# VectorE, ScalarE and SyncE in source order through projections and time mixing, and attention's loads on SyncE

## Chip, cores, metric

One core of one Trainium2 chip. The metric is the device time of one execution, in us. Engines: TensorE (PE; its weight loads are PEld), VectorE (DVE), ScalarE (ACT), GpSimd (POOL), SyncE (SP, which here only issues DMAs).

## What is computed

A decoder block on x of 2048 x 1024 float32:

```python
xn = rms_norm(h, ln_attn_pre); proj = xn @ w_in            # 1792 columns time mixing, 1536 attention
y_rwkv = rwkv7_mix(proj[..., :RWKV_COLS], ...)             # 8 heads of 64; a state carried from token to token
o = diff_attention(dq, dk, dv, lam, slopes)                # 4 heads, two softmaxes each, causal, ALiBi
h = h + rms_norm(concat(y_rwkv, o) @ w_out)
u = causal_dwconv(rms_norm(h) @ w_up); h = h + rms_norm((gelu(gate) * val) @ w_down)
```

In `rwkv7_mix` the projections are first mixed with those of the token before (`shift`), decay and learning rate come from small low-rank products, keys are normalised, and the state is `state * w + sa (kk a) + v k`. The output gets a norm over each head and a gate.

## The kernel before

Matrix products run in three float32r passes (high and low parts of both sides, made by ScalarE's cast and VectorE's subtraction: `split_weight`, `transpose_half`).

**Projections** (`Proj`). `w_in` is taken in 26 blocks of 128 columns, 14 for time mixing (`NRW`) and 12 for attention (`NDF`: q, k, v of each head); tokens in two halves of two groups of 512 (`GRP`). `product` makes one block for one group, 24 matmuls in 8 steps, and after each step `pace.tick()` runs what is due. `plan` gives the order: half 0's blocks 2 to 13, half 1's 26 blocks, half 0's 12 attention blocks, and before a change of half the last two blocks as (a,0), (b,0), (b,1), (a,1). `weights` loads and splits a block when the one before it is first used. `turn` reloads normalised rows (`xr`) and transposes them for the next half. Results are written to DRAM by GpSimd (`rw`, `qq`, `kk`, `vT`).

**Time mixing** (`Rwkv.group`) is a generator for 128 tokens. Its `yield`s are offsets in ticks from its start; one group starts every `PITCH` = 34 ticks, from the product (0, 13, 1) on, so about three groups are in work at once, and there are 16. Within a group: low-rank products, scans and key norm (offsets 5 to 20); the masks, that is `M` (24, 26); its 32 x 32 blocks to DRAM (`adr`) and back (`ab`); a substitution of 31 steps on VectorE, `tmp = X * ab; X += tmp` (34 to 46, called the loop here); `X` through DRAM (`xdr`) to `x1t`, `bdx` and `M`; from `JOIN` = 64 the halves are joined (`xp`), and from 71 the state is carried over two chunks of 64 (`rp`, `sp`, `yp`, `up`); then the norm (`mp`, `vs`), the gate (`gp`) and the store to `mix`, up to offset 105. `power` makes an inverse root on GpSimd, `turned` transposes it and copies it to `rT`, `spread` multiplies `rT` out over the partitions.

**Attention** (`Attn.steps`) walks units of 128 queries of a head: `scores` of unit i and `output` of unit i - 2. K, V and Q are loaded when first needed, K and Q by GpSimd, V by SyncE. While it runs, `w_out` is loaded and split (source place: unit 6).

**Then** the output projection and the MLP, to the end.

**The order.** Every engine runs its instructions in one order. For TensorE, from the start to the end of time mixing, this is the order of the source (`tc.manual_schedule(engines={PE})`). For VectorE, ScalarE, SyncE and GpSimd, and for all engines from attention on, a planner sets it, from its own costs and the order of the source, and can draw work ahead when its tile is free. Tiles of a pool are reused one by one (`reuse_waits="tile"`).

Of the kernel before, what the change touches and what calls it, by code (L numbers as in the profile page):

```python
# [18 lines left out]
P = 128  # L19
# [58 lines left out]
def transpose_split(nc, cx, ps, xn, xh, xl, t, tag, bufs):  # L78

    g, o = divmod(t * P, GRP)  # L80
    for hf in range(2):
        transpose_half(nc, cx, ps, xn[:, hf * 512:hf * 512 + 512], xh[g], xl[g], t, hf, o, tag, bufs)
# [75 lines left out]
class Proj:  # L158


    def __init__(self, tc, nc, cx, I, pool, pace):
# [7 lines left out]
        self.x, self.w = {}, {}  # L169
# [37 lines left out]
    def rows(self, t, hf, xn, x):  # L207
        transpose_half(self.nc, self.cx, self.cx.ps, xn[:, hf * 512:hf * 512 + 512], *x, t, hf, t * P % GRP, *self.cx.ra)
# [27 lines left out]
    def turn(self, half, g, every):  # L236
# [4 lines left out]
        i = 0  # L241
        for t in range(g * 4, g * 4 + 4):
            for hf in range(2):
                xr = self.pool.tile([P, 512], F32, name=f"xr{use}_{t}_{hf}", tag="xr", bufs=3)
                nc.sync.dma_start(xr, cx.xn[half * (HALF // P) + t][:, hf * 512:hf * 512 + 512])
                transpose_half(nc, cx, cx.ps, xr, xh, xl, f"{use}_{t}", hf, t * P % GRP, *cx.mm)
                i += every
                yield i

    def weights(self, half, cb):  # L250
# [4 lines left out]
        nc.sync.dma_start(wr, self.w_in[:, :, wc * P:(wc + 1) * P])  # L255
        wh = pool.tile([P, KB, P], F32R, name=f"wh{half}_{cb}", tag="wh", bufs=2)
        wl = pool.tile([P, KB, P], F32R, name=f"wl{half}_{cb}", tag="wl", bufs=2)
        split_weight(nc, wr, wh, wl)
        self.w[half, cb] = wh, wl

    def tmp(self, n):
        pool = self.pool
        return (lambda dt: pool.tile([P, GRP], dt, name=f"e1_{n}", tag="e1", bufs=2),
                lambda dt: pool.tile([P, GRP], dt, name=f"e2_{n}", tag="e2", bufs=1))

    def shift(self, half, cb, g, pp):

        nc, cx = self.nc, self.cx
        t0 = half * HALF + g * GRP
        e1, e2 = self.tmp(f"{half}_{cb}_{g}")  # L270
        t1, xs = e1(F32), e2(F32)
        c1 = self.carry[:, cb:cb + 1]
        m1 = self.mu[:, cb:cb + 1]
        nc.scalar.activation(t1, pp, AF.Copy, scale=self.mu1[:, cb:cb + 1])
# [25 lines left out]
    def evict(self, half, cb, g, pp, n):  # L300
# [13 lines left out]
        nc.scalar.activation(hi, pp, AF.Copy, scale=sc)  # L314
        nc.vector.scalar_tensor_tensor(lo, pp, sc, hi.bitcast(F32), op0=ALU.mult, op1=ALU.subtract)
# [6 lines left out]
    def plan(self, stages):  # L322
# [3 lines left out]
        after = dict(zip(order, order[1:]))  # L326
        self.weights(*order[0])
        seen = set()
        for i, (half, blocks) in enumerate(stages):
            turns = i + 1 < len(stages) and stages[i + 1][0] != half  # L330
# [4 lines left out]
            for j, (cb, g) in enumerate(todo):  # L335
                if (half, cb) not in seen:
# [14 lines left out]
PITCH, JOIN = 34, 64  # L351
# [88 lines left out]
class Rwkv:  # L440
# [31 lines left out]
    def group(self, g):  # L472
# [19 lines left out]
        nc.sync.dma_start(vv, src[8:12, :, tok].rearrange("b p t -> p b t"))  # L492
        yield 5
# [8 lines left out]
        nc.gpsimd.tensor_tensor(k0, c4(kr), ch(v["nk_k"]), op=ALU.mult)  # L502
# [4 lines left out]
        nc.scalar.activation(tha, za, AF.Tanh, scale=0.5)  # L507
        nc.vector.tensor_scalar(th, th, 1.0, None, op0=ALU.add)
# [7 lines left out]
        sb = self.power(rn, ALU.max, 1e-24, f"kk{g}")  # L516
        pe, pc = cx.pe, T([P, 4, NC], "pc", 3)
# [3 lines left out]
        nc.vector.tensor_copy(pc, pe[:, :, :, 64])  # L521
        kt = T([P, 4, RG], "t_c")
        for hb in range(4):
            nc.scalar.activation(kt[:, hb], tha[:, hb], AF.Identity, bias=v["ka1"][:, hb:hb + 1],
                                 scale=v["kah"][:, hb:hb + 1])
        kp = kr
        tt(kp, kr, kt, op=ALU.mult)
        BK = T([P, 4, NC, 2, 64], "BK")
# [3 lines left out]
        rk = T([P, 4, RG], "t_b")  # L532
        nc.gpsimd.tensor_tensor(c4(rk), rr, ch(v["r_k"]), op=ALU.mult)
        nc.vector.tensor_scalar(tha, tha, -0.5, -0.5, op0=ALU.mult, op1=ALU.add)
# [41 lines left out]
        X = T([P, 8, 32], "X")  # L576
        nc.sync.dma_start(X, cx.xinit)
# [19 lines left out]
        for j in range(31):  # L597
            if j % 5 == 0:
                yield 34 + 2 * (j // 5)
# [60 lines left out]
        yield at  # L660
        for c in range(NC):
# [7 lines left out]
            yield at + 9 * c + 3  # L669
# [7 lines left out]
            yield at + 9 * c + 6  # L677
# [13 lines left out]
            yield at + 9 * c + 9  # L691


        at += 21
        sg = T([P, RG], "sg")
        nc.sync.dma_start(sg, src[13, :, tok])
        mp = U([P, 4, RG], "mp")
        nc.tensor.matmul(mp, cx.ones2, ybv, start=True, stop=True)
        stt(ybv, mp, -1.0 / 64, ybv, op0=ALU.mult, op1=ALU.add)
        sq = T([P, 4, RG], "t_a")  # L700
# [14 lines left out]
        yield at + 13  # L715
# [4 lines left out]
        nc.sync.dma_start(cx.mix[g * RG // GRP][0:4, :, tok].rearrange("b p t -> p b t"), ybv)  # L720
# [53 lines left out]
class Attn:  # L774


    def __init__(self, tc, nc, cx, pool, ps):
        self.tc, self.nc, self.cx, self.pool, self.ps = tc, nc, cx, pool, ps
# [9 lines left out]
    def load_k(self, h, g):  # L788
        nc, cx = self.nc, self.cx
        gs = slice(g * GRP, (g + 1) * GRP)  # L790
        ka = self.T([P, 2, GRP], "ka", f"{h}{g}", 5, F32R)
        kb = self.T([P, 2, GRP], "kb", f"{h}{g}", 5, F32R)
# [5 lines left out]
        vt = self.T([P, GRP], "vtl", f"{h}{g}", VB)  # L798
        nc.sync.dma_start(vt, cx.vT[h, :, gs])
# [4 lines left out]
        self.heads[h, g] = (ka, kb, v)  # L804

    def load_q(self, h, g):
# [5 lines left out]
        nc.gpsimd.dma_start(qa, src[0:128, :, gs])  # L812
        nc.gpsimd.dma_start(qb[0:66], src[64:130, :, gs])
        self.qs[h, g] = (qa, qb)

    def scores(self, h, qb):
        nc, cx = self.nc, self.cx
        g, qi = divmod(qb, QG // P)
        if qb % 4 == 0:
            self.load_k(h, qb // 4)  # L820
        if qi == 0:
            self.load_q(h, g)
# [42 lines left out]
        self.live[h, qb] = (E[0], sc)  # L865

# [261 lines left out]

def block_kernel(tc, I, out):
    nc = tc.nc  # L1130
    cx = Ctx()
    with ExitStack() as st:
# [18 lines left out]
        with pool("pj", "left") as pp:  # L1151
# [4 lines left out]
            with tc.manual_schedule(engines={mybir.EngineType.PE}):  # L1156
# [14 lines left out]
        banks.close()  # L1171
        cx.ps = st.enter_context(tc.tile_pool(name="ps2", bufs=4, space=PSUM, reuse_waits="tile"))
        cx.mm, cx.ra, cx.rc = ("mm", 4), ("ra", 2), ("rc", 2)
        of = OutFfn(tc, nc, cx, I, out)
# [33 lines left out]
```

## Time and profile before

| | us |
|---|---|
| three runs | 3174.24, 3181.33, 3188.11 |
| median | 3181.33 |
| profiled execution, its own time | 3190.99 |
| its span in the profile | 3189.3 |
| mean granted clock of TensorE | 0.972 of 2.4 GHz |

The projections and time mixing run from about 180 to 1086 us, attention from there to some 1530 us, output projection and MLP to the end. In the rows below, `PE x L1 <- DVE y L2` is a wait of TensorE's instruction at line 1 that writes x for VectorE's at line 2 that writes y; a wait in brackets stands before the instruction, with what ended it.

### The profile page before, as it was taken

The numbers are of one execution on the slowest core, as the hardware profiler recorded it, in microseconds if no ns is written. First come the engines' busy times: TensorE is split into PE (matmuls) and PEld (weight loads), VectorE is DVE, ScalarE is ACT, GpSimd is POOL, SyncE is SP. The second block draws the span as 40 slices with busy tenths as digits, with TensorE's granted clock in tenths as the row PEclk, the third lists the DMA queues.
The fourth block names the chain that finished last, engine by engine and source line by source line (L and its number), as shares of the span: only waits on it lengthen the run. The fifth ranks groups of instructions, "written<-read, shape, count | busy, mean of one in ns | idle before, by whom it ended". The sixth has DMA issues, their size and how long they took to land.

```text
span 3189.3 us, 46522 instructions
## 1 busy us (share of the span) xinstructions
PE 3016.8 (95%) x17411; PEld 2459.6 (77%) x17411; DVE 1937.6 (61%) x4935; ACT 1168.1 (37%) x2292; POOL 448.9 (14%) x641
## 2 busy tenths in 40 slices
PE   7998999999999789999999999999999999999998
PEld 6876777777777577778788888888887788888886
DVE  6366667576766367778455455555557455555556
ACT  5242333332432367778333322222224322222223
POOL 4211111222221334432100000000000000000002
PEclk9998999999999889999999999999999999999999
DMA  8443333434443635542444111111114311111112
GB/s 301 120 139 87 88 87 96 114 98 113 132 119 89 156 71 96 92 80 57 136 155 176 53 40 60 47 47 47 40 60 136 103 51 43 52 49 52 47 34 86
DMA packets 367075, 290.84 MB, mean 91 GB/s; under 512 B 114511, under 2 KB 317874, under 8 KB 366850
## 3 DMA queue, kind: packets, MB, share of 16 engines
q1 hardware_dynamic: 325554, 211.46, 22.7%
q0 software_dynamic: 38992, 72.21, 9.6%
q10 hardware_dynamic: 2304, 4.20, 0.3%
q8 instruction: 138, 2.26, 0.3%
q14 instruction: 87, 0.71, 0.1%
HBM read 208.91 MB, written 78.07 MB: 90 GB/s over the span
## 4 chain that ended last, share of the span: by engine, by line
PE 70%; DVE 10%; issue 7%; DMA 6%; ACT 2%; SPq 2%; POOL 2%; DVEq 0%; POOLq 0%; ACTq 0%
PE fp L103 10%; PE fp L105 10%; PE fp L104 10%; PE dn L104 5%; PE dn L103 5%; PE dn L105 5%; PE pp L293 3%; PE op L883 3%; PE pp L294 2%; PE pp L295 2%; PE po L103 2%; PE po L105 2%; PE po L104 2%; DVE xtmp L612 1%; DVE X L614 1%
## 5 line engine op out<-in xcount | busy, mean ns | idle before, releaser
L1066 DVE TENSOR_TENSOR acc<-dn,acc 128x512 f32<-128x512 f32 x320 | 211.3, 686 | 224.5 <-PE dn L105 222.1
L103 PE MATMUL fp<-f1h,uh 128*128 128x512 f32 x704 | 275.4, 391 | 5.1 <-DVE fcarry L1031 5.1
L105 PE MATMUL fp<-f1h,ul 128*128 128x512 f32 x704 | 275.2, 391 | 0.0
L104 PE MATMUL fp<-f1l,uh 128*128 128x512 f32 x704 | 275.1, 391 | 0.0
L104 PE MATMUL dn<-dl,gh 128*128 128x512 f32 x704 | 275.1, 391 | 0.0
L103 PE MATMUL fp<-f0h,uh 128*128 128x512 f32 x704 | 274.2, 389 | 0.0
L103 PE MATMUL dn<-dh,gh 128*128 128x512 f32 x704 | 272.4, 391 | 1.9 <-DVE acc L1066 1.9
L105 PE MATMUL fp<-f0h,ul 128*128 128x512 f32 x704 | 274.1, 389 | 0.0
L104 PE MATMUL fp<-f0l,uh 128*128 128x512 f32 x704 | 274.0, 389 | 0.0
L105 PE MATMUL dn<-dh,gl 128*128 128x512 f32 x704 | 264.1, 391 | 0.0
L844 DVE TENSOR_SCALAR_CACHE_REDUCE E<-sp 128x512 f32<-128x512 f32 (+3 forms) x320 | 186.1, 605 | 69.1 <-PE sp L842 37.8
L97 DVE TENSOR_TENSOR ul<-ur,uh 128x1024 fp32r<-128x1024 f32 x88 | 107.7, 1225 | 188.0 <-ACT uh L96 188.0
L1027 DVE SCALAR_TENSOR_TENSOR u<-fp,cvA,u 128x511 f32<-128x511 f32 x176 | 131.3, 746 | 120.1 <-ACT u L1025 120.1
L96 ACT CAST dh<-dr 128x1024 fp32r<-128x1024 f32 x44 | 44.4, 1047 | 385.0 <-PE dn L105 384.0
L612 DVE TENSOR_TENSOR xtmp<-X,ab 128x60 f32<-128x60 f32 (+24 forms) x496 | 109.1, 220 | 118.5 <-DMA ab<-adr 80.3
L883 PE MATMUL op<-V,at 128*128 128x128 f32 x1088 | 159.5, 288 | 9.1 <-ACT at L879 8.7
L883 PEld LDWEIGHTS op<-V,at 128*128 128x128 f32 x1088 | 144.7, 199 | 24.2 <-ACT at L879 18.4
L839 PE MATMUL sp<-ka,qa 128*128 128x512 f32 (+3 forms) x320 | 137.9, 443 | 26.4 <-DMA qa<-qq 22.8
L1025 ACT ACTIVATE u<-fp,cvB 128x512 f32<-128x512 f32 x176 | 136.5, 777 | 62.7 <-PE fp L105 62.6
L103 PEld LDWEIGHTS fp<-f1h,uh 128*128 128x128 f32 x704 | 132.7, 189 | 33.4 <-issue 5.5
L853 ACT ACTIVATE E<-E,asc 128x1024 f32<-128x1024 f32 (+7 forms) x160 | 153.4, 962 | 11.1 <-DVE asc L849 10.5
L103 PEld LDWEIGHTS dn<-dh,gh 128*128 128x128 f32 x704 | 132.6, 188 | 30.3 <-DVE acc L1066 2.3
(344 smaller groups left out, 7045.1 us busy)
## 6 DMA issues: line engine op xcount, KB each, us to landing
ur<-in_w_up SPq DMA_DIRECT2D x88, 512.0 KB
wr<-in_w_in SPq DMA_DIRECT2D x52, 512.0 KB
dr<-in_w_down SPq DMA_DIRECT2D x44, 512.0 KB
rw<-e POOLq DMA_DIRECT2D x56, 256.0 KB, 2.9
x<-in_x SPq DMA_DIRECT2D x16, 512.0 KB
xn<-x POOLq DMA_DIRECT2D x16, 512.0 KB, 6.6
xr<-xn SPq DMA_DIRECT2D x32, 256.0 KB
ab<-adr SPq DMA_DIRECT2D x64, 128.0 KB
```

What stands on the lines that cost most here:

```text
L97: nc.vector.tensor_tensor(wl, wr, wh.bitcast(F32), op=ALU.subtract)
L103: nc.tensor.matmul(out, lh(kb), rh(kb), start=(kb == 0), stop=False)
L104: nc.tensor.matmul(out, lh(kb), rl(kb), start=False, stop=False)
L105: nc.tensor.matmul(out, ll(kb), rh(kb), start=False, stop=(kb == n - 1))
L612: tt(tv, X[:, 0:n, j:j + 1].broadcast_to([P, n, w]), ab[:, j:j + 1, j + 1:32].broadcast_to([P, n, w]), op=ALU.mult)
L839: nc.tensor.matmul(sp[:, 0:n], qa[:, c, qs], ka[:, c, 0:n], start=True, stop=False)
L844: nc.vector.tensor_scalar(e[ch * GRP // EW][:, eo:eo + n], sp[:, 0:n], -1.0, None, op0=ALU.mult, op1=ALU.min, accum_out=mx[:, ch:ch + 1])
L853: nc.scalar.activation(e[i][:, 0:n], e[i][:, 0:n], AF.Exp, bias=nm, scale=-1.0, accum_out=z)
L883: nc.tensor.matmul(op, at[:, q, :], v[:, q, :], start=(kb == 0), stop=(kb == qb))
L1025: nc.scalar.activation(u, pp, AF.Identity, bias=wb(b), scale=w2(b))
L1027: stt(u[:, 1:GRP], pp[:, 0:GRP - 1], w1(b), u[:, 1:GRP], op0=ALU.mult, op1=ALU.add)
L1066: nc.vector.tensor_tensor(acc[:, t, ds_], po, acc[:, t, ds_], op=ALU.add)
```

## The change

- VectorE, ScalarE and SyncE take the order of the source too, from the product (0, 13, 1) until time mixing has ended.
- What they issue gets ticks of its own. VectorE's half of a transpose's split, of a token shift and of a q or k eviction comes one step or one tick after ScalarE's (`later`). Weights are fetched two blocks ahead and split 3 ticks after the block before is first used, or 2 ticks into the last product of a stage. `xr` is fetched two ahead. All three stages end with the order (a,0), (b,0), (b,1), (a,1). The `e2` buffers are two.
- In `group` the key product on GpSimd moves to offset 3; scans, `kt`, `kp`, BK and the masks get offsets of their own; `xinit` is loaded before the blocks go to DRAM; the loop starts at 35; `JOIN` is 59; the two chunks follow at 10 ticks; `vs` is spread at +14 in place of +12; `sg` is loaded at `JOIN` + 7; the last step stays at 105. The store to `mix` goes from SyncE to GpSimd.
- Attention's K and Q are loaded by SyncE, a unit ahead of their use, those of head 0 before the drain of time mixing; V is transposed where it was.

```diff
 def transpose_half(...):
-    nc.vector.tensor_tensor(xl[:, ks, dst], pt, xh[:, ks, dst].bitcast(F32), op=ALU.subtract)
+    return lambda: nc.vector.tensor_tensor(xl[:, ks, dst], pt, xh[:, ks, dst].bitcast(F32), op=ALU.subtract)
...
+    def later(self, at, f, *args):
+        def step():
+            f(*args)
+            yield from ()
+        self.pace.add(step(), self.pace.now + at)
...
     def shift(self, half, cb, g, pp):
         nc.scalar.activation(t1, pp, AF.Copy, scale=self.mu1[:, cb:cb + 1])
+        self.later(1, self.shifted, half, cb, g, pp, t1, xs)
...
     def plan(self, stages):
+        self.fetch(*order[0])
+        self.fetch(*order[1])
         self.weights(*order[0])
...
-            if turns:
-                a, b = blocks[-2:]
-                todo[-4:] = [(a, 0), (b, 0), (b, 1), (a, 1)]
+            a, b = blocks[-2:]
+            todo[-4:] = [(a, 0), (b, 0), (b, 1), (a, 1)]
...
-                    if (half, cb) in after:
-                        self.weights(*after[half, cb])
+                    if k + 2 < len(order):
+                        self.fetch(*order[k + 2])
+                    if cb != b:
+                        split(k + 1, 3)
+                if j == len(todo) - 1:
+                    split(place[half, b] + 1, 2)
...
-PITCH, JOIN = 34, 64
+PITCH, JOIN = 34, 59
...
+            yield 25 + 2 * c
             mv = M[:, c].rearrange("p (b e) x -> p e b x", e=2)
             for e, sx in ((0, se), (1, so)):
                 tt(mv[:, e], sx, mk, op=ALU.mult)
+        X = T([P, 8, 32], "X")
+        nc.sync.dma_start(X, cx.xinit)
...
-                yield 34 + 2 * (j // 5)
+                yield 35 + 2 * (j // 5)
...
-            yield at + 9 * c + 3
+            yield at + 10 * c + 3
...
-        yield at + 12
+        yield at + 14
         self.spread(rl, cx.rT[1])
         tt(ybv, ybv, rl, op=ALU.mult)
+        yield at + 15
...
-        nc.sync.dma_start(cx.mix[g * RG // GRP][0:4, :, tok].rearrange("b p t -> p b t"), ybv)
+        nc.gpsimd.dma_start(cx.mix[g * RG // GRP][0:4, :, tok].rearrange("b p t -> p b t"), ybv)
...
-    def load_k(self, h, g):
+    def fetch_k(self, h, g):
+        vt = self.T([P, GRP], "vtl", f"{h}{g}", VB)
+        nc.sync.dma_start(vt, cx.vT[h, :, gs])
+        if g == 0:
+            self.load_q(h, 0)
+        ka = self.T([P, 2, GRP], "kab", f"a{h}{g}", 10, F32R)
+        kb = self.T([P, 2, GRP], "kab", f"b{h}{g}", 10, F32R)
         src = cx.kk[h].rearrange("c r t -> r c t")
         for i in range(2):
-            nc.gpsimd.dma_start(ka[64 * i:64 * i + 64], src[0:64, :, gs])
-        nc.gpsimd.dma_start(kb[0:66], src[64:130, :, gs])
+            nc.sync.dma_start(ka[64 * i:64 * i + 64].bitcast(F32), src[0:64, :, gs])
+        nc.sync.dma_start(kb[0:66].bitcast(F32), src[64:130, :, gs])
...
         self.live[h, qb] = (E[0], sc)
+        h2, q2 = divmod(h * (S // P) + qb + 1, S // P)
+        if q2 % 4 == 0 and h2 < NH:
+            self.fetch_k(h2, q2 // 4)
+        if qi == 1 and q2:
+            self.load_q(h, g + 1)
...
+ORDERED = {mybir.EngineType.DVE, mybir.EngineType.Activation, mybir.EngineType.SP}
...
                     if at == (0, NRW - 1, 1):
                         for i in range(NGRP):
                             pace.add(rw.group(i), pace.now + 3 + PITCH * i)
+                        break
+                with tc.manual_schedule(engines=ORDERED):
+                    for at in products:
+                        pass
+        of = OutFfn(tc, nc, cx, I, out)
+        with pool("at", "left") as ap:
+            at = Attn(tc, nc, cx, ap)
+            at.fetch_k(0, 0)
+            with tc.manual_schedule(engines=ORDERED | {mybir.EngineType.PE}):
                 pace.drain()
```

## Rows read from the trace of the kernel before

**Rows 1.** The page, busy time: engine, busy us (share), instructions.

```profile
PE 3016.8 (95%) x17411; PEld 2459.6 (77%) x17411; DVE 1937.6 (61%) x4935; ACT 1168.1 (37%) x2292; POOL 448.9 (14%) x641
```

**Rows 2.** Windows by stage: length, busy us of each engine (instructions), clock, DMA, GB/s.

```profile
180.00:1086.00 906.00, 834.97 (x6917) 650.45 (x6917) 593.65 (x1782) 303.86 (x612) 192.61 (x238) 0.95 0.39 103
1086.00:1140.00 54.00, 25.90 (x95) 19.96 (x96) 23.23 (x73) 22.82 (x51) 21.95 (x34) 0.56 1.12 213
1140.00:1500.00 360.00, 332.88 (x2268) 284.06 (x2268) 279.31 (x1043) 267.94 (x685) 131.97 (x199) 0.97 0.41 79
...
1570.00:3189.30 1619.30, 1596.51 (x7060) 1317.63 (x7058) 919.18 (x1747) 472.58 (x739) 40.48 (x52) 0.99 0.22 70
```

**Rows 3.** TensorE's waits, 180 to 1080 us: us in total, times, longest.

```profile
PE vs L470 <- DVE rT L466: 22.6, 8, 4.3
PE rp L666 <- DVE X L614: 11.1, 7, 3.4
PE xp L641 <- DMA x1t<-xdr: 11.0, 1, 11.0
PE xt L89 <- DMA xr<-xn: 8.1, 4, 4.5
```

**Rows 4.** VectorE's waits, 180 to 1080 us.

```profile
DVE xtmp L612 <- DMA ab<-adr: 80.3, 12, 10.9
```

**Rows 5.** VectorE's groups by line, 180 to 1086 us: busy us, mean ns, idle before.

```profile
L612 DVE TENSOR_TENSOR xtmp<-X,ab 128x60 f32<-128x60 f32 (+24 forms) x496 | 109.1, 220 | 118.5 <-DMA ab<-adr 80.3 <-DMA bda<-M 13.7 <-DMA X<-xinit 12.8
L614 DVE TENSOR_TENSOR X<-X,xtmp 128x60 f32<-128x60 f32 (+24 forms) x496 | 107.6, 217 | 12.1
...
L566 DVE TENSOR_TENSOR M<-se,mask 128x512 f32<-128x512 f32 x32 | 22.0, 688 | 26.5 <-PE so L563 26.5
...
L668 DVE TENSOR_TENSOR kv<-rp,kv 128x256 f32<-128x256 f32 x32 | 13.5, 420 | 5.1 <-PE rp L666 5.1
```

**Rows 6.** Timeline, first group's loop, VectorE, then TensorE: start us, us.

```profile
217.91 0.68 DVE L566 TENSOR_TENSOR M<-so,mask 128x512 f32<-128x512 f32 x1
...
226.40 0.19 DVE L612 TENSOR_TENSOR xtmp<-X,ab 128x31 f32<-128x31 f32 x1 [4.46 <-DMA ab<-adr]
...
259.69 0.17 DVE L614 TENSOR_TENSOR X<-X,xtmp 128x8 f32<-128x8 f32 x1
...
267.92 0.60 PE L641 MATMUL xp<-ident,x1t 32*128 32x32 f32 x4 [10.99 <-DMA x1t<-xdr]
```

**Rows 7.** Timeline of the turn into attention, SyncE's queue, then TensorE.

```profile
1086.53 4.48 SPq L944 DMA_DIRECT2D wor<-in_w_out  x5
1091.12 0.86 SPq L799 DMA_DIRECT2D vtl<-vT  x2
...
1102.48 1.09 PE L802 MATMUL vp<-ident,vtl 128*128 128x128 f32 x4 [16.53 <-DMA vtl<-vT]
...
1114.49 1.05 PE L877 MATMUL tp<-ident,E 128*128 128x128 f32 x3 [0.45 <-DVE E L864]
...
1128.40 0.90 PE L839 MATMUL sp<-ka,qa 128*128 128x512 f32 x2 [7.70 <-DMA qa<-qq]
```

**Rows 8.** Timeline, first and last matmul row of the last product, TensorE.

```profile
1078.60 0.39 PE L293 MATMUL pp<-x6h,wh 128*128 128x512 f32 x1
...
1085.57 0.39 PE L295 MATMUL pp<-x6h,wl 128*128 128x512 f32 x1
```

**Rows 9.** Attention: TensorE's waits 1140 to 1500 us, and the first in time.

```profile
PE sp L839 <- DMA qa<-qq: 13.6, 3, 4.6
...
1217.80 0.76 POOL L812 DMA_DIRECT2D qa<-qq  x1 [0.18 <-issue]
...
1221.32 1.86 PE L839 MATMUL sp<-ka,qa 128*128 128x384 f32 x4 [4.55 <-DMA qa<-qq]
```

**Rows 10.** Windows of 10 us at the second head's start.

```profile
1210.00:1220.00 10.00, 5.58 (x48) 5.11 (x46) 5.15 (x17) 6.16 (x16) 5.67 (x9) 0.96 1.59 206
1220.00:1230.00 10.00, 8.69 (x51) 7.99 (x52) 2.27 (x8) 1.44 (x3) 2.89 (x5) 0.70 1.16 154
```

More of the change, by code (lines that the diff above doesn't have):

```diff
@@ L240, in turn, with fetch @@
         use = self.uses
[L241 to L250, printed above, removed]
+        rows, low = [], None
+        def fetch():
+            t, hf = g * 4 + len(rows) // 2, len(rows) % 2
+            rows.append(self.pool.tile([P, 512], F32, name=f"xr{use}_{t}_{hf}", tag="xr", bufs=3))
+            nc.sync.dma_start(rows[-1], cx.xn[half * (HALF // P) + t][:, hf * 512:hf * 512 + 512])
+        fetch()
+        fetch()
+        for i in range(8):
+            t, hf = g * 4 + i // 2, i % 2
+            if i < 6:
+                fetch()
+            do = transpose_half(nc, cx, cx.ps, rows[i], xh, xl, f"{use}_{t}", hf, t * P % GRP, *cx.mm)
+            if low:
+                low()
+            low = do
+            if i == 7:
+                low()
+            yield (i + 1) * every
+    def fetch(self, half, cb):
         nc, pool = self.nc, self.pool
@@ L255, in weights @@
         nc.sync.dma_start(wr, self.w_in[:, :, wc * P:(wc + 1) * P])
+        self.raw[half, cb] = wr
+    def weights(self, half, cb):
+        nc, pool = self.nc, self.pool
+        if (half, cb) not in self.raw:
+            self.fetch(half, cb)
         wh = pool.tile([P, KB, P], F32R, name=f"wh{half}_{cb}", tag="wh", bufs=2)
         wl = pool.tile([P, KB, P], F32R, name=f"wl{half}_{cb}", tag="wl", bufs=2)
-        split_weight(nc, wr, wh, wl)
+        split_weight(nc, self.raw.pop((half, cb)), wh, wl)
         self.w[half, cb] = wh, wl
+    def later(self, at, f, *args):
[3 more added lines that the diff above has]
+        self.pace.add(step(), self.pace.now + at)
     def tmp(self, n):
@@ L314, in evict, with lower @@
         nc.scalar.activation(hi, pp, AF.Copy, scale=sc)
+        self.later(1, self.lower, half, h, kind, t0, pp, hi, lo, sc)
+    def lower(self, half, h, kind, t0, pp, hi, lo, sc):
+        nc, cx = self.nc, self.cx
         nc.vector.scalar_tensor_tensor(lo, pp, sc, hi.bitcast(F32), op0=ALU.mult, op1=ALU.subtract)
@@ L325, in plan, with split @@
         order = [(half, cb) for half, blocks in stages for cb in blocks]
-        after = dict(zip(order, order[1:]))
+        place = {b: i for i, b in enumerate(order)}
+        seen = set()
+        self.fetch(*order[0])
+        self.fetch(*order[1])
         self.weights(*order[0])
-        seen = set()
+        def split(i, at):
+            if i < len(order):
+                self.later(at, self.weights, *order[i])
         for i, (half, blocks) in enumerate(stages):
-            turns = i + 1 < len(stages) and stages[i + 1][0] != half
+            end = i + 1 == len(stages)
+            turns = not end and stages[i + 1][0] != half
             todo = [(cb, g) for cb in blocks for g in range(2)]
-            if turns:
-                a, b = blocks[-2:]
-                todo[-4:] = [(a, 0), (b, 0), (b, 1), (a, 1)]
+            a, b = blocks[-2:]
+            todo[-4:] = [(a, 0), (b, 0), (b, 1), (a, 1)]
             for j, (cb, g) in enumerate(todo):
+                k = place[half, cb]
                 if (half, cb) not in seen:
                     seen.add((half, cb))
-                    if (half, cb) in after:
-                        self.weights(*after[half, cb])
+                    if k + 2 < len(order):
[4 more added lines that the diff above has]
+                    split(place[half, b] + 1, 2)
                 yield half, cb, g
@@ L516, in group @@
         sb = self.power(rn, ALU.max, 1e-24, f"kk{g}")
+        kt = T([P, 4, RG], "t_a")
+        for hb in range(4):
+            nc.scalar.activation(kt[:, hb], tha[:, hb], AF.Identity, bias=v["ka1"][:, hb:hb + 1],
+                                 scale=v["kah"][:, hb:hb + 1])
+        rk = T([P, 4, RG], "t_b")
+        nc.gpsimd.tensor_tensor(c4(rk), rr, ch(v["r_k"]), op=ALU.mult)
+        yield 9
         pe, pc = cx.pe, T([P, 4, NC], "pc", 3)
@@ L520, in group @@
         nc.scalar.activation(ip, cum, AF.Exp, scale=0.5 * DECAY)
[L521 to L525, printed above, removed]
         kp = kr
         tt(kp, kr, kt, op=ALU.mult)
+        nc.vector.tensor_scalar(tha, tha, -0.5, -0.5, op0=ALU.mult, op1=ALU.add)
+        yield 11
+        nc.vector.tensor_copy(pc, pe[:, :, :, 64])
         BK = T([P, 4, NC, 2, 64], "BK")
@@ L803, in load_k @@
         nc.scalar.copy(v, vp)
-        self.heads[h, g] = (ka, kb, v)
+        self.heads[h, g][2] = v
     def load_q(self, h, g):
@@ L1169, in block_kernel @@
                             pace.add(rw.group(i), pace.now + 3 + PITCH * i)
-                pace.drain()
[L1171 to L1174, printed above, removed]
-        cx.const = base
-        with pool("at", "left") as ap:
-            for i, _ in enumerate(Attn(tc, nc, cx, ap, cx.ps).steps(range(NH))):
+                        break
[7 more added lines that the diff above has]
+            with tc.manual_schedule(engines=ORDERED | {mybir.EngineType.PE}):
+                pace.drain()
+            banks.close()
+            cx.ps = at.ps = st.enter_context(tc.tile_pool(name="ps2", bufs=4, space=PSUM, reuse_waits="tile"))
+            cx.mm, cx.ra, cx.rc = ("mm", 4), ("ra", 2), ("rc", 2)
+            cx.const = base
+            for i, _ in enumerate(at.steps(range(NH))):
                 if i == ALONE:
```

58 lines of the change are left out of this document (28 added, 30 removed).

## The prediction

> **What bounds the kernel now.** I read the page first. TensorE is busy for 95% of the span [rows 1], so a change in issue order can only return time in which TensorE stands or runs at its lower clock. The windows by stage say where that is [rows 2]. From 1570 us on (MLP) TensorE is busy 1596.51 of 1619.30 us, and the change touches nothing there. Three stretches are left:
>
> - 180 to 1086 us, projections with time mixing woven in ("the stage" below): 834.97 busy of 906.00, so 71 us idle, at a granted clock of 0.95. Between 1.0 (2.4 GHz) and 0.5 (1.2 GHz) that is about a tenth of the stage, 91 us, at the lower level, which gives back 45 us at most.
> - 1086 to 1140 us, the turn into attention: 25.90 busy of 54.00 at 0.56.
> - 1140 to 1500 us, attention: 332.88 of 360.00 at 0.97.
>
> Next the waits of TensorE in the stage [rows 3]. The largest is spreading the normalisation's factors (`vs`) until VectorE has copied `rT`, 22.6 us in 8 waits; then the state products `rp` behind the substitution loop on `X`, 11.1 us in 7; one wait of 11.0 us for `x1t`, in the first group; 8.1 us for reloaded rows `xr`. No engine is full there. VectorE is 593.65 busy of 906 (66%), yet stood 80.3 us in 12 waits on `ab`, the round trip of the blocks through DRAM [rows 4]. So VectorE stands early in a group and is late afterwards: this is a matter of order, and the part the change rewrites. The first group shows it. Its loop starts when `ab` lands at 226.40 and needs 13.5 us of work (109.1 + 107.6 us over 16 groups [rows 5]), but ends at 259.9 with the next group's work between, and `xp` waits until 267.92 [rows 6].
>
> **The turn, first part.** TensorE's first wait after the projections is 16.53 us for `vtl`, whose load SyncE issues at 1091.12 behind five loads of `w_out`; later come 7.70 us for `qa`, which GpSimd issues [rows 7]. The change puts the first K, V and Q loads into SyncE's order ahead of the tail, and its new order of the last four products frees the half's first x tiles (group 0) 16 ticks before the projections end, about 14 us at 0.87 us a tick there (the last product, eight ticks, ran from 1078.6 to 1085.6 [rows 8]). If the buffers of attention lie over those tiles, about 1.4 MB land before TensorE needs them (at the window's 213 GB/s [rows 2], 7 us). TensorE's work in the turn is 25.90 x 0.56 = 14.5 us at full clock, and 16 us at attention's own share of 92%. So 54 - 16 = 38 us is the most. The pipeline must still fill (first `vp` to first `tp` took from 1102.48 to 1114.49 [rows 7], at half clock and with two waits; I take 5 us) and the `w_out` splits, now hidden in the idle time, compete with the first units (3 us). I take 30. If instead the loads must wait for the last product, 7 us more go: 23 at least without another fault.
>
> **Attention's loads on SyncE.** Later heads wait 13.6 us in three waits for `qa` [rows 9], and the clock is 0.70 in the 10 us around the first of them [rows 10], up to 3 us lost there, 9 in three, of which I count 6 as the rest was idle. In the traced case GpSimd issues that `qa` at 1217.80, behind other loads and a power, and TensorE goes on at 1221.32 [rows 9]. The new code asks for Q and K at the end of the unit before, in a queue that waits for no arithmetic. Bounds: nothing (the transfers themselves are what is late) and 13.6 plus the 6 us of clock. I take 10, near the upper half, because the issue and not the transfer is the last event. The Trainium skill, "DMA: Bandwidth & Descriptors", section "Issuing engines are not separate DMA queues", says that another issuing engine saves only the sequencer's time to start a transfer. By that rule alone this term would be near nothing; the trace's `qa` row, 3.5 us from issue to use, leaves both readings open, and it has a rival below.
>
> **The stage in source order.** Nothing is removed from TensorE's stream; its products and ticks are the same (PITCH 34, each group still ends at offset 105). A tick is 906/624 = 1.45 us: 78 products of eight from the point where groups start. What is rewritten is when VectorE, ScalarE and SyncE take each step. I lay VectorE's steps on the 34 ticks that groups repeat in, with durations of [rows 5] and 0.42 to 0.69 us for the 256- and 512-wide steps:
>
> - Ticks 1 to 14: the loop 13.5, and beside it the next group's scans, BK, rT and products (about 7) and the last group's state steps (about 3), plus splits and token shift (about 2.5): 26 us in 14 ticks = 20.3 us. VectorE ends 6 us, four ticks, late.
> - Tick 17: 3.5 us (k0, b2, BK, k0); ticks 25 and 27: the masks, 1.4 us each; the other 20 ticks hold 13 us in 29. The lateness is gone before the masks.
>
> So with the new ticks: the masks of tick 27 are done near 28; in the first group their end at 218.6 to `ab` at 226.40 is 7.8 us, 5.4 ticks, so `ab` is there at 33.5 and the loop is due at 35: VectorE's 80 us of standing should mostly go. The loop's last step is issued at 47 and done near 51 or 52; from its end at 259.9 to `x1t` usable at 267.92 is 8 us, 5.5 ticks [rows 6], so 57.5 against JOIN 59 (64 before). It fits, by 2 us. The normalisation's spread comes two ticks later, in ticks where VectorE isn't late: 18 of its 22.6 us return. Of the 11.1 us of `rp`, 8 (the first chunk now comes ahead of the loop). Of `x1t`, all 11. Of `xr`, 5 (two loads ahead now). Sum 42.
>
> New waits: `rT` of the key norm falls on tick 13, where VectorE is 6 us late, and its spread is due at 17, 5.8 us on: I charge 1 us a group, 16. Evictions and shifts that now stand in line behind a step that waits: 10, between 0 and the 16 x 2 us which four such steps of 0.5 us would make. Net idle returned 42 - 26 = 16 us of 71, and the same share of the 45 us of clock, 10. The stage gives 26. Its ends: all of 71 + 45 back is out of reach; a loss is the rival below. The `mix` store moved to GpSimd costs it one issue of some 0.6 us a group, hidden in a stage where it is busy 192.61 of 906 [rows 2]; what stands behind it is the power of a later group, several ticks off. Weights fetched two blocks ahead have two buffers, so nothing new waits there.
>
> **Sum.** 30 + 10 + 26 = 66 us. The profiled execution took 3190.99 us, 1.7 of it outside the span; less 66 that is 3125. It lies 9.7 above the median of the runs, 3181.33, by which I state the time: 3115. A measurement here tells about 0.5%, 16 us, from no change.
>
> **Rivals.**
> 1. *The stage gains far more.* For: weight loads are busy 650.45 of 906 there (72%) and 1317.63 of 1619.30 (81%) in the MLP; at the MLP's share the stage would take 650/0.81 = 800. Against: small matmuls with dependencies don't pack like the MLP's. Two thirds of that gap, 70 us in place of 26, and the upper ends of the other terms (38 and 20) give 128: 3053. The Trainium skill, "Perfetto Trace Analysis", section "Identifying the Most-Contended Engine", takes weight-load share and not matmul share for TensorE's distance from its limit; by it the stage has this 106 us of room where busy time shows 71.
> 2. *The stage returns nothing,* its new waits equal to the old ones: 40 us from the turn and the loads, 3141.
> 3. *The loads' move does nothing*, the transfers being the limit (DMA share 1.59 in the 10 us in which a head's loads run [rows 10]): no 10, and the turn 23: 49 us, 3132.
> 4. *Slower: VectorE in source order is too late for JOIN 59.* Place: `xp` waiting for `x1t`. Slack is 2 us. Every us beyond it stops TensorE in each of 16 groups, 16 us, and the clock falls behind it. To lose more than 16 us net of the 40 from turn and loads, the stage must lose 56, so 3.5 us a group: a loop that ends some 12 us late in place of 6. At 5 us a group it is 80 - 40, 3221. For it: VectorE has 37 us of work in 49 and an in-order engine also stands for every product of the same tick. Against: when TensorE stops, VectorE catches up, so the lateness limits itself.
>
> **How the numbers follow.** Forecast 0.50 (3080 to 3150), rival 1 0.13, rival 2 0.14, rival 3 0.05, something between 3165 and 3197 0.07, rival 4 0.11. Faster by over 0.5% 0.82, within 0.07, slower 0.11. The range 3065 to 3185 leaves out the far half of rival 1 and rival 4, and some of the case between.
>
> **What would show it.** Right: TensorE starts attention within about 10 us of the last product, with no wait for `vtl`; no wait of 4.6 us for `qa` at a head; VectorE's waits on `ab` under 30 us in place of 80; waits of `vs` on `rT` mostly gone, some of `n` on `rT` new; clock over 0.96 in the stage. Wrong: many waits of `xp` on `x1t` (rival 4), a stage of 900 us or more (rival 2), the first `vtl` issued after the last product (the turn's lower bound).

## The result and the profile after

The changed kernel takes 3212.65 us (median of 4 runs, 3209.28 to 3220.49) against 3184.72 us for the kernel before beside it: ratio 1.0089, 95% interval [1.0067, 1.0111]. It is slower by 0.9%; 3115 us was forecast, 2% under. The profiled execution has a span of 3213.7 us, 24.4 over that of before.

The windows by stage of the changed kernel (length, busy us of PE, PEld, DVE, ACT and POOL with instructions, clock, DMA share, GB/s), beside [rows 2]:

```profile
180.00:1113.70 933.70, 850.10 (x6915) 647.52 (x6914) 619.57 (x1774) 302.62 (x612) 191.83 (x250) 0.95 0.39 102
1113.70:1155.00 41.30, 28.59 (x121) 20.73 (x120) 28.22 (x100) 23.18 (x55) 7.79 (x12) 0.67 0.97 257
1155.00:1548.00 393.00, 353.98 (x2411) 306.38 (x2410) 294.80 (x1067) 282.94 (x719) 72.86 (x118) 0.96 0.29 77
1548.00:3213.00 1665.00, 1639.58 (x7233) 1352.67 (x7233) 941.14 (x1782) 488.96 (x777) 45.05 (x60) 0.99 0.23 72
```

The loss is in the first line. For a sharper cut I take, in each trace's timeline, the start of the first `zw` product, of the last step (three matmuls) of the last projection product, and of attention's last `op`. From `zw` to the last product ("the stage") before took 903.1 us and after 933.6, 30.5 longer. From there to the last `op` ("turn and attention") before took 439.7 and after 434.4, 5.3 shorter. What follows takes 1664.4 and 1666.0. The same three stretches are used below for every run. Each is from one execution, and such an execution can lie up to 11 us from the median of its kernel: that of before took 3190.99 us, where the medians of before beside the runs below are 3180.35 to 3186.03. In the first run below, whose stage is coded as before, the stage took 892.1. So a difference of under some 10 us between two stretches says little, and a gain against 903.1 is rather an upper end; the medians decide.

TensorE's waits in the stage after (us in total, times, longest), beside [rows 3], and two of VectorE's groups, beside [rows 5]:

```profile
PE sp L722 <- DVE kv L718: 19.3, 13, 3.7
PE xt L89 <- DMA xr<-xn: 18.3, 4, 11.6
PE n L513 <- DVE rT L509: 14.9, 9, 2.8
PE mp L746 <- DVE ybv L740: 10.0, 10, 2.0
...
PE zw L543 <- DMA twx<-rw: 1.7, 1, 1.7
```

```profile
L660 DVE TENSOR_TENSOR xtmp<-X,ab 128x60 f32<-128x60 f32 (+24 forms) x496 | 115.5, 233 | 18.8 <-DMA ab<-adr 4.9
...
L614 DVE TENSOR_TENSOR M<-se,mask 128x512 f32<-128x512 f32 x32 | 22.0, 686 | 21.0 <-PE so L610 21.0
```

The waits that the change aimed at are gone: no `xp` on `x1t`, no `vs` on `rT`, and VectorE's standing at `ab` went from 80.3 us [rows 4] to 4.9. Others of like size stand in their place: `sp` on `kv`, which the forecast had not named, and `xr`, whose waits were to shrink from 8.1 us to 3 and are 18.3, one of them 11.6.

Idle time is only half of the loss. From the first `zw` to the end of the last product TensorE is idle for 69.0 us before and 83.6 after, and busy for 835.0 and 850.8, with 6917 and 6920 matmuls in the trace. Of the longer busy time the clock is a part: over windows of 5 us, what the granted clock lacks to 2.4 GHz adds up to 42.6 us before and 49.5 after.

What tells more is SyncE's own queue, of which the forecast read no wait at all. Its waits in the stage, after:

```profile
SPq L665 <- DVE rT L509: 238.5, 14, 21.1
SPq L710 <- PE gp L768: 142.0, 15, 11.2
SPq L621 <- DVE M L614: 69.7, 30, 17.1
```

Before, at the load that is L710 after:

```profile
SPq L696 <- PE gp L718: 82.1, 13, 13.2
```

Then GpSimd and ScalarE, after:

```profile
POOL AR L537 <- DMA kr<-rw: 57.3, 11, 13.3
```

```profile
ACT t_a L547 <- POOL AR L537: 88.3, 15, 7.5
```

L710 loads `sg`, the gate's input. It has one buffer, read by `gp` at the end of a group. Before, the load came near that end in the source, and SyncE in the planner's order stood at it too, 82.1 us. The change put it at JOIN + 7, tick 66 of a group. The group ahead started 34 ticks earlier and reads the buffer at its tick 105, which is tick 71 of this one. So SyncE stands some five ticks in every group but the first: 142.0 us in 15 waits. The loads of the next group to start, due at tick 68, stand behind it, as SyncE's rows after show (start us, us), then the other engines' rows of the same moment:

```profile
635.64 0.42 SPq L266 DMA_DIRECT2D wr<-in_w_in  x1
645.57 0.34 SPq L710 DMA_DIRECT2D sg<-rw  x1
645.96 0.50 SPq L526 DMA_DIRECT2D twx<-rw  x1
646.50 0.60 SPq L527 DMA_DIRECT2D alx<-rw  x1
647.20 0.55 SPq L529 DMA_DIRECT2D kr<-rw  x1
```

```profile
644.38 1.16 PE L768 MATMUL gp<-sg,gup 128*128 128x128 f32 x8
...
649.63 1.13 PE L543 MATMUL zw<-twx,lora 65*128 65x128 f32 x8 [0.80 <-DVE X L662]
...
651.42 1.03 POOL L537 TENSOR_TENSOR AR<-kr,rkder 128x512 f32<-128x512 f32 x1 [2.96 <-DMA kr<-rw]
652.49 0.63 ACT L547 ACTIVATE t_a<-AR 128x512 f32<-128x512 f32 x1 [7.13 <-POOL AR L537]
...
653.64 0.43 DVE L553 TENSOR_SCALAR t_b<-t_b 128x512 f32<-128x512 f32 x1 [2.40 <-ACT t_b L549]
```

SyncE stands from 636.06 on and issues `sg` when `gp` has read the buffer, at 645.5. Then `kr` lands late, GpSimd's `k0` waits for it, ScalarE in source order stands 7.13 us at the square of `k0` with the tanh of the decay and whatever else it has behind that, and VectorE's scans come after. TensorE's own list of waits puts 1.7 us to `twx` and most of the rest to VectorE; this chain begins in a queue. How far it carries the loss is tested below.

### The profile page after: what moved, and what is told of

Its sections match the earlier page's. It is cut to its first block, busy times and chain, and to the rows that moved or that the text cites. A ratio compares the mean times of both kernels' runs of the same rounds, so it can differ in the third digit from the quotient of the medians.

```text
span 3213.7 us, 46506 instructions
## 1 busy us (share of the span) xinstructions
PE 3035.9 (94%) x17411; PEld 2462.4 (77%) x17411; DVE 1970.6 (61%) x4935; ACT 1164.5 (36%) x2292; POOL 372.5 (12%) x545
## 4 chain that ended last, share of the span: by engine, by line
PE 78%; DVE 10%; DMA 5%; issue 3%; ACT 2%; SPq 1%; POOL 1%; DVEq 0%; POOLq 0%; ACTq 0%
PE fp L103 10%; PE fp L105 10%; PE fp L104 10%; PE pp L321 5%; PE dn L104 5%; PE dn L103 5%; PE dn L105 5%; PE pp L322 4%; PE pp L323 4%; PE op L943 3%; DVE xtmp L660 2%; PE po L103 2%; PE po L105 2%; PE po L104 2%; DVE X L662 2%
## 5 line engine op out<-in xcount | busy, mean ns | idle before, releaser
L894 PE MATMUL sp<-kab_a,qa 128*128 128x512 f32 (+3 forms) x320 | 141.5, 444 | 27.2 <-DMA qa<-qq 15.7
L104 PEld LDWEIGHTS fp<-f1l,uh 128*128 128x128 f32 x704 | 133.1, 189 | 28.0
```

The source lines that it names most:

```text
L104: nc.tensor.matmul(out, lh(kb), rl(kb), start=False, stop=False)
L894: nc.tensor.matmul(sp[:, 0:n], qa[:, c, qs], ka[:, c, 0:n], start=True, stop=False)
```

## The experiments

The question is which part is the loss: VectorE in source order (near the forecast's rival 4, and the theory of the first expectations), SyncE in source order, ScalarE's order, the attention part, or the ticks. That SyncE's loss goes through `sg` and `xr` was read after the first four runs, which cut the change along those lines.

**Attention part alone.** Before, with attention's loads on SyncE and the early first loads; the stage as it was.

```
+            at.fetch_k(0, 0)
...
-        nc.gpsimd.dma_start(qa, src[0:128, :, gs])
+        nc.sync.dma_start(qa.bitcast(F32), src[0:128, :, gs])
```

> The kernel before with the attention part of the change alone (K, V and Q loaded by SyncE a unit ahead, head 0's first loads before the drain of time mixing; the last products in the old order; all engines but TensorE ordered by the planner as before). Theory 'transfers bound': in the changed kernel the stretch from the last product to the last head took 434 us against 439, so the part is worth 5 us or less: 0.995 to 1.003 of before. Rival 'the move works, but the new stage spoils it': 20 us or more faster, 0.994 or less, with the waits of scores on qa under 5 us in all.

Measured: 3195.95 us, ratio 1.0038 [1.0018, 1.0058]; turn and attention 446.6 us. Alone it is a loss, not a gain, which neither expectation named. The trace shows SyncE issuing the first `vtl` at 1081.44, behind six loads of `w_out` and four of the convolution's constants, and TensorE waiting 12.53 us for it.

**Stage part alone.** The changed stage, with attention as before.

> The changed kernel with attention as before (K and Q loaded by GpSimd when first needed, after the drain). Theory 'the stage is the loss': the products end near 1114 us as in the changed kernel, and the time is 28 us above before, 1.007 to 1.012. Rival 'the two parts meet' (SyncE's queue or the buffers of attention delay the stage): the products end by 1095 us and the time is within 10 us of before.

Measured: 3225.80 us, 1.0143 [1.0123, 1.0164]; stage 935.5. The whole loss is in the stage part; beside the new stage the attention part is a gain, of 1.0143 to 1.0089.

**The planner's order kept, new ticks.** After, with TensorE alone in source order.

```
-                with tc.manual_schedule(engines=ORDERED):
-                    for at in products:
-                        pass
+                for at in products:
+                    pass
...
-            with tc.manual_schedule(engines=ORDERED | {mybir.EngineType.PE}):
+            with tc.manual_schedule(engines={mybir.EngineType.PE}):
```

> The changed kernel with all its ticks, loads and buffers, but VectorE, ScalarE and SyncE ordered by the planner as before; TensorE in source order. Theory 'source order': VectorE, standing in line for products of the same tick, is what makes kv, rT and mp late; without it the stage falls from 934 us back to 906 or below. Rival 'ticks': the new offsets in TensorE's own order (JOIN 59, chunks 10 apart) come too early for any order, and the stage stays at 925 us or more.

Measured: 3161.96 us, 0.9944 [0.9924, 0.9964]; stage 880.8, 22.3 less than before. The new ticks are good (18.6 us by the medians, the attention part with them), and the order of the three engines costs 53 us in the stage on top of them.

**VectorE alone in source order.**

```
-ORDERED = {mybir.EngineType.DVE, mybir.EngineType.Activation, mybir.EngineType.SP}
+ORDERED = {mybir.EngineType.DVE}
```

> The changed kernel with only VectorE in source order; ScalarE and SyncE ordered by the planner. Theory 'source order on VectorE': the stage stays at 925 us or more, the waits of sp on kv and of n on rT stay (34 us in the changed kernel). Rival 'SyncE in source order': its queue, which stood 238 us for the loop's result, delays xr and the blocks; with the planner's order of SyncE the stage falls by 15 us or more and the waits on xr (18 us) go to under 9.

Measured: 3167.21 us, 0.9966 [0.9946, 0.9986]; stage 886.0, so VectorE's order alone is not the loss. TensorE's waits in it are `n` on `rT`, which the forecast charged, and two that it had not named; together 42.7 us, about what the planner's order spent on `x1t` (40.4 us, below):

```profile
PE n L513 <- DVE rT L509: 20.9, 14, 2.8
PE mp L746 <- DVE ybv L740: 11.6, 13, 2.0
PE sp L722 <- DVE kv L718: 10.2, 10, 1.5
```

**VectorE with ScalarE, and VectorE with SyncE.** The same line with `Activation`, or `SP`, added.

> The changed kernel with VectorE and ScalarE in source order, SyncE by the planner. The stage was 934 us with three engines in order and 886 with VectorE alone. Theory 'SyncE': its source order costs the 48 us, so this run has a stage of 885 to 900 us and a time below before's by 5 us or more. Rival 'ScalarE': ScalarE's order costs them, the stage stays at 920 us or more.

> The changed kernel with VectorE and SyncE in source order, ScalarE by the planner. Theory 'SyncE': stage of 920 us or more, xr waits of about 18 us in all, SyncE standing over 200 us for the loop's result. Rival 'ScalarE': stage below 900 us.

Measured: with ScalarE 3173.0 us, 0.9976 [0.9963, 0.9990], stage 889.5; with SyncE 3196.49 us, 1.0048 [1.0026, 1.0071], stage 921.3. SyncE's order is the loss. ScalarE's adds to it: it costs 0.10% with SyncE left to the planner (0.9966 to 0.9976) and 0.41% beside SyncE in source order (1.0048 to 1.0089), though the intervals hardly part the two. The run with ScalarE also shows that standing alone isn't the loss: there SyncE, in the planner's order, stands 104.6 us at `sg` too. What it costs depends on which loads are behind it: around the same moment of that run the next group's `kr` is issued at 601.92, ahead of `sg` at 629.52.

**JOIN 64 with the planner's order.** The largest wait left in the run with the planner's order was `xp` on `x1t`, 40.4 us in 9. This one gives it five more ticks.

```
-PITCH, JOIN = 34, 59
+PITCH, JOIN = 34, 64
```

> The changed kernel with all engines but TensorE ordered by the planner, and JOIN back at 64. With JOIN 59 the only large wait of this order was xp on x1t, 40 us in 9. Theory 'JOIN 59 is too early for the planner's order': five ticks are 7 us a group, the wait goes under 12 us, the stage from 881 to 845 to 860 us, the time to 3130 to 3142. Rival 'the wait moves on' to the state steps or vs: stage above 870 us, time above 3150.

Measured: 3170.17 us, 0.9970 [0.9959, 0.9980], stage 889.5. The wait moved on:

```profile
PE xp L689 <- DMA x1t<-xdr: 20.7, 5, 10.7
PE rp L716 <- DVE X L662: 18.1, 7, 3.5
PE rp L716 <- DVE xtmp L660: 8.6, 4, 4.6
```

**Two buffers for `sg`.** After, with all three engines in source order.

```
-        sg = T([P, RG], "sg")
+        sg = T([P, RG], "sg", 2)
```

> The changed kernel, all three engines in source order, with two buffers for the gate's input sg in place of one. In the changed kernel SyncE stands before the load of sg, 142 us in 15 waits, until the group before has used its sg five ticks later, and the next group's loads stand behind it. Theory 'sg': the load no longer stands, key and low-rank inputs come in time, the scans and all after them start earlier, and the stage falls by 20 us or more, to 914 or less. Rival 'the loop's result': SyncE's long wait is for the loop (238 us), behind which xr and weights stand, and sg's is only its continuation: stage within 8 us of 934.

Measured: 3185.28 us, 1.0018 [1.0006, 1.0029]; stage 902.2, 31.4 less than after. One buffer is most of the loss against before. TensorE's idle time from the first `zw` to the end of the last product falls from 83.6 us to 67.6 and its busy time from 850.8 to 835.4, at a mean granted clock of 0.96 in place of 0.95. The wait of `t_a` on GpSimd is no longer among ScalarE's larger ones.

How much of the chain that began at `sg` bears the cost? In the changed kernel `kr` is issued 1.5 us ahead of its group's first `zw` product and `k0` is done 3.3 us behind it; the tanh starts 3.8 us behind it and VectorE's step after the tanh (L553) 4.5 (medians of 16 groups, from the timelines). With two buffers these are 10.6 ahead, 5.3 ahead, 1.1 and 3.3 behind. So the start of the chain is right. The rest isn't shown: in the run with VectorE and SyncE in order, where ScalarE is free to take the tanh first, `k0` is as late (3.4 us behind `zw`), the tanh comes 1.2 us and L553 2.5 us behind, about as early as with two buffers or earlier, and the stage still took 921.3. There the late `k0` must cost by another way, which stays open. SyncE's waits with two buffers:

```profile
SPq L665 <- DVE rT L509: 330.9, 14, 26.1
SPq L621 <- DVE M L614: 69.6, 32, 14.7
SPq L842 <- PE pp L323: 33.6, 1, 33.6
```

SyncE now stands 330.9 us at L665, the store of the substitution loop's result, which waits for VectorE (238.5 us there and 142.0 at `sg` in the changed kernel). In most groups TensorE waits for nothing behind it. At the turn of the halves it does, for the reloaded rows `xr`, which stand behind the store (issued at 809.88 after 9.3 us of standing) and the transfers that follow it; SyncE's rows, then TensorE's:

```profile
818.89 1.91 SPq L680 DMA_DIRECT2D M<-xdr  x4
820.90 0.87 SPq L246 DMA_DIRECT2D xr<-xn  x2
```

```profile
823.76 1.12 PE L89 MATMUL xt<-ident,xr 128*128 128x128 f32 x4 [12.10 <-DMA xr<-xn]
```

**And the `xr` loads on GpSimd.**

```
-            nc.sync.dma_start(rows[-1], cx.xn[...][:, hf * 512:hf * 512 + 512])
+            nc.gpsimd.dma_start(rows[-1], cx.xn[...][:, hf * 512:hf * 512 + 512])
```

> The changed kernel with two buffers for the rows of ln's statistics (sg) and the ten loads of transposed rows (xr) issued by GpSimd. Theory 'what is left after sg is the xr loads standing behind the loop's store at SyncE': TensorE's waits on xr (14.3 us) fall under 3, the stage goes from 902 to about 889 us, and the time to 3168 to 3178 us, some 0.4% under the kernel before. Rival 'GpSimd in its planner's order makes xr late too': xr waits stay over 8 us and the stage stays at about 900, the time at 3185. Rival 'ticks and VectorE are the rest': xr waits go and the waits on rT, kv and mp grow by as much, stage 898 to 902.

Measured: 3175.81 us, 0.9978 [0.9966, 0.9991]; stage 894.7. TensorE's waits for `xr` fall from 14.3 us to 1.3. With both loads out of the way the kernel with all three engines in source order is as fast as the one with SyncE left to the planner (0.9976).

**Later ticks.** What TensorE waits for in that run is VectorE: `n` 17.0 us, `sp` 15.5, `mp` 12.5. So five ticks were moved later, once on top of the last run, once on the run with VectorE alone in source order.

```
-        yield 17
+        yield 19
...
-            yield at + 10 * c + 3
+            yield at + 10 * c + 4
...
-            yield at + 10 * c + 6
+            yield at + 10 * c + 7
...
-        at += 22
+        at += 24
```

(and the bonus from 20 to 21.)

The last of these edits doesn't move `mp`. The line `at += 24` stands ahead of `mp` in the source, but the `yield` before both is `at + 10 * c + 10`, so `mp` stays at offset 86; only what comes behind `mp` moves by two. The step that makes its input, at `at + 10 * c + 7` with c = 1, moves from 82 to 83.

> As the kernel with two sg buffers and xr on GpSimd, with five ticks moved later: the key's spread by 2, the bonus by 1, the scores and the pairs by 1 each, the output's transposes by 2. Theory 'the ticks ask for results before VectorE has them, and VectorE has room': the waits n on rT (16 us), sp on kv (15), mp on its rows (11) fall to a third and the stage comes to 855 to 870 us, the time to 3140 to 3155. Rival 'VectorE's order is itself the limit': the waits move to other tiles, their sum stays within 10 us, and the stage stays at 885 us or above, time 3165 or more.

> The new ticks and VectorE alone in source order, SyncE and ScalarE in the planner's, one sg buffer, with the same five ticks moved later. Theory 'the ticks are too early for VectorE': the stage falls from 886 us to 860 to 870, the time from 3167 to 3140 to 3150. Rival 'VectorE's order is the limit': 3160 to 3170, with the waits moved on.

Measured: 3204.40 and 3204.42 us, both 1.0065 [1.0045, 1.0084]; stages 920.6 and 922.8. Where the reader was moved its wait fell: in the first run `n` on `rT` from 17.0 us to 1.0, `sp` on `kv` from 15.5 to 9.8. `mp`, whose input was moved and which was not, rose from 12.5 to 48.5 (and to 50.6 in the second run):

```profile
PE mp L746 <- DVE ybv L740: 48.5, 14, 5.2
```

In each of the 16 groups 12 product matmuls (four ticks) lie between the last `yp` and `mp` in the run before, and 9 (three ticks) in these two. TensorE's row for one group in the run before, then in the first of these, with VectorE's rows there:

```profile
506.02 1.12 PE L746 MATMUL mp<-ybv,ones 128*128 128x512 f32 x2 [0.80 <-DVE ybv L740]
```

```profile
513.12 1.40 PE L746 MATMUL mp<-ybv,ones 128*128 128x512 f32 x2 [2.30 <-DVE ybv L740]
```

```profile
510.03 0.27 DVE L508 CAST rT<-n 8x128 fp32r<-8x128 f32 x1
...
511.86 0.41 DVE L735 TENSOR_TENSOR st<-state,up 128x256 f32<-128x256 f32 x1
512.31 0.42 DVE L736 TENSOR_TENSOR state<-st,pc 128x256 f32<-128x256 f32 x1
512.65 0.41 DVE L740 TENSOR_TENSOR ybv<-yp,ybv 128x256 f32<-128x256 f32 x1
```

VectorE's order at this place is the same in both runs, and L740 starts 2.62 us behind `rT` in both (505.55 behind 502.93 in the run before); only TensorE comes to `mp` a tick sooner after `yp`. Sixteen ticks of 1.45 us are 23 us, by estimate, of the 36 by which this wait grew; the rest is open. So these two runs don't decide between the theories: the ticks with `mp` moved as well were not run. No tick setting tried with VectorE in source order beat the planner's order.

**The ticks alone.** Before with the new ticks only: planner's order, attention's loads as before. With the run of the planner's order it shows what the attention part is worth beside the new ticks.

> The new ticks in the stage with VectorE, ScalarE and SyncE in the planner's order, and attention as before: its loads of Q, K and V and the turn into it. It differs from the 0.9944 run (planner's order, attention's loads moved) by the attention part alone. Theory 'attention's loads on SyncE bring nothing': within 0.3% of that run, 3155 to 3170 us, turn and attention 430 to 440 us. Theory 'they cost what they cost beside the old stage (0.4%)': 3145 to 3153. Rival 'they bring the 12 us that the stage part showed without them': 3172 to 3178, turn and attention 443 to 447.

Measured: 3177.44 us, 0.9976 [0.9963, 0.9989], stage 881.0, turn and attention 444.3 (432.8 with the attention part). So the rival is right: beside the new ticks the attention part brings 0.3%, with intervals that just meet, and 11.5 us in these two profiles. The turn in this run, then in the run with the attention part (TensorE's rows):

```profile
1066.64 1.09 PE L852 MATMUL vp<-ident,vtl 128*128 128x128 f32 x4 [5.53 <-DMA vtl<-vT]
1082.36 1.19 PE L889 MATMUL sp<-ka,qa 128*128 128x128 f32 x4 [14.63 <-DVE wol L97]
```

```profile
1061.02 0.60 PE L859 MATMUL vp<-ident,vtl 128*128 128x128 f32 x4
1062.64 0.73 PE L894 MATMUL sp<-kab_a,qa 128*128 128x128 f32 x4 [1.02 <-DVE e L347]
1066.93 0.48 PE L895 MATMUL sp<-kab_b,qb 66*128 66x128 f32 x1 [3.57 <-DMA kab_b<-kk]
```

The early loads need both parts. On the new ticks, in the run with the attention part, SyncE issues the first `vtl` at 1048.38, 12 us ahead of the end of the last product; on the old ones it came after it.

## Why the prediction was wrong

**The step that failed: "Weights fetched two blocks ahead have two buffers, so nothing new waits there."** It was the forecast's only sentence on what SyncE in source order could hold up in the stage, and put that at nothing. It looked at one of the loads in that queue. The `sg` load, moved from the end of a group to tick 66, was in the diff and was not laid against its one buffer, although the tick arithmetic needs nothing but the code: read at 105 by a group that starts 34 ticks earlier is 71, five ticks after the load is due. Nor was `xr` laid against the loop's store ahead of it: 5 of its 8.1 us were to return, and it waits 18.3. Measured in its place: SyncE's order costs 1.13% (0.9976 to 1.0089), 36 us. Put right, step by step (stage of one profile each, ratio of medians):

| kernel | stage, us | ratio to before |
|---|---|---|
| before | 903.1 | 1 |
| new ticks and attention part, planner's order | 880.8 | 0.9944 |
| VectorE in source order | 886.0 | 0.9966 |
| ScalarE too | 889.5 | 0.9976 |
| SyncE too, `sg` and `xr` out of its way | 894.7 | 0.9978 |
| SyncE too, only `sg` out of its way | 902.2 | 1.0018 |
| all three: the changed kernel | 933.6 | 1.0089 |

So 0.71% of the time is `sg`, 0.40% `xr`, 0.02% the rest of SyncE's order, 0.10% ScalarE, 0.22% VectorE; the last three are near what such a comparison can tell. The shares hold for this order of taking things out; ScalarE's is larger beside SyncE's order, as said. The two buffers show what `sg` costs, and that `kr` and `k0` come late by it; by which links this reaches TensorE is not shown.

**The stage, forecast to give 26 us.** Without SyncE's order the stage gives 13.6 us (903.1 to 889.5), with VectorE alone in order 17.1, with the planner's order 22.3: at most half to two thirds of this term. Even its sign isn't safe, since the medians of the first of these kernels and of before, turn and attention included, differ by 7.4 us only. It was right that `ab` stops holding VectorE, that JOIN 59 fits with VectorE in source order (no wait of `xp` on `x1t`: rival 4 is out, though it came slower), and that `n` waits for `rT`: 14.9 to 20.9 us where 16 were charged. Not foreseen were `sp` on `kv` and `mp` on `ybv`, 22 us together with VectorE alone in order, where the forecast allowed 10 for everything else. The forecast that TensorE's clock would go over 0.96 failed: it was granted 0.95, as before.

**The turn, forecast to give 30 us.** Its mechanism was right: TensorE's first scores start at 1114.29, right behind the last product, whose last row starts at 1113.70, with no wait for `vtl`. Its size was not. From the first scores to the last `op` attention takes 420 us before and 434 after: the loads of `w_out` and their splits, hidden in the turn's idle time before, run beside the first units (window 1113.70 to 1155.00: DMA share 0.97, TensorE busy 28.59 of 41.30 at 0.67). The forecast charged 3 us for that competition and 5 for the filling of the pipeline, and attention took 14 longer; that the competition is the cause is read from these windows, no run tests it. One load was still late, because the tile of `kab_b` is free only after the last product; it is issued at 1114.13, and TensorE waits 4.32 us for it.

**Attention's loads, forecast to give 10 us.** They give next to nothing. TensorE's waits on `qa` after, in the stretch that answers to [rows 9]:

```profile
PE sp L894 <- DMA qa<-qq: 11.5, 5, 3.5
```

That is 2.1 us under the 13.6 of before. The step that failed is "in a queue that waits for no arithmetic": SyncE's queue waits for TensorE to let go of the buffers, from 1155 to 1548 us:

```profile
SPq L869 <- PE sp L897: 119.8, 13, 18.8
SPq L849 <- PE sp L894: 47.7, 4, 15.8
```

At the second head it stands 15.8 us for a tile of `kab` and then issues twelve loads of K and four of Q between 1220.10 and 1235.2; the `qa` load of 1233.16 stands in that line. Rival 3 was right in the outcome: the burst of loads is late, whoever issues it. Whether the transfers are the limit, as it said, isn't shown: the DMA share is 0.87 and 0.96 in the two windows of 10 us from 1220, but the loads also start late. The Trainium skill, "DMA: Bandwidth & Descriptors", section "Issuing engines are not separate DMA queues", says that another issuing engine saves only the time to start a transfer; the waits left, 11.5 us of 13.6, agree.

**Rival 1** found nothing in its favour: the stage never came under 880.8 us. The weight-load share by which the Trainium skill, "Perfetto Trace Analysis", section "Identifying the Most-Contended Engine", reads TensorE's room was 72% before and 69% after. The busy time of the weight loads is nearly the same, 650.45 and 647.52 us, so here the share falls because the stage is longer; it says nothing of what the change could win.

**The sum.** Stage +30.5 in place of -26; turn, attention and loads -5.3 in place of -40; 91 us of the 97.6 between 3115 and 3212.65. SyncE's order is 36 of these, turn, attention and loads 35; what is left is about the gain that the stage was to give. So SyncE's step is what made the kernel slower, and little over a third of the miss: with SyncE left to the planner the kernel is 0.24% under before, 7.4 us by the medians and not 66.

**Best version.** Of all that ran, the new ticks with the planner's order for VectorE, ScalarE and SyncE are fastest: 3161.96 us, 0.9944 of before.

## What to carry to other kernels

When a queue is put in source order, list every load in it with the tick at which it is issued, the number of its buffers and the tick at which the last reader lets go; any load that comes before its buffer is free holds back all that stand behind it, and a buffer more can be worth more than the whole reordering. Read the queues' own waits as well as the engines': TensorE's waits here named VectorE, and the loss began at SyncE. When a step's tick is moved, look behind which `yield` its reader stands: here the step moved a tick later, its reader stayed, and the wait grew by 36 us. Compare stretches of single executions only where they differ by more than such an execution strays from its median, and try the parts one at a time before the whole.

## What the runs showed of the hardware

A load whose destination isn't free keeps SyncE from issuing later loads that could run: 142.0 us in 15 waits, with 31.4 us of stage behind them. The length of such standing says nothing of its price: behind 330.9 us at the loop's store in the run with two `sg` buffers TensorE waited 14.3 us for `xr`, 12.10 of it at one place, and with 104.6 us at the same `sg` in the planner's order the stage was 44 us shorter than in the changed kernel. Before, SyncE stood there for 82.1 us.
